# Preparing the operand sums of a third feed-forward unit per layer with accumulating transfers, with other places for the units and their tails

## The chip, the cores and the metric

The kernel runs on one core of one Trainium2 chip. The metric is the device time of one execution in microseconds (us). A core has five engines that run side by side: TensorE (PE in the profile; its weight loads are PEld), VectorE (DVE), ScalarE (ACT), GpSimd (POOL) and SyncE (SP, which only issues transfers). Sixteen DMA engines move data for all of them.

## The reference, cut to what matters

Two layers over 256 positions of width 2048. Layer 0 mixes with pooling and attention, layer 1 with a matrix memory (mLSTM). Each layer ends in the same feed-forward block, which is where the change lies:

```python
def conv_ffn(x, w_up, conv_w, conv_b, w_down):
    u = x @ w_up                                  # 256x2048 @ 2048x11264
    up = jnp.pad(u, ((0, 0), (1, 1), (0, 0)))
    u = c[0] * up[:, :-2] + c[1] * up[:, 1:-1] + c[2] * up[:, 2:] + conv_b
    gate, val = jnp.split(u, 2, axis=-1)
    return (jax.nn.silu(gate) * val) @ w_down     # 256x5632 @ 5632x2048
# every layer: x = x + mixer(rms_norm(x)); x = x + conv_ffn(rms_norm(x), ...)
```

All of it is float32.

## The kernel before

**Products.** A float32 product is made of three reduced products: each weight tile is split into a high part `hl[:, 0]` (a copy that rounds to `fp32r`, line 164, on ScalarE) and a low part `hl[:, 1]` (the difference, line 165, on VectorE), and high x high, high x low and low x high are summed in PSUM (the helper `mm`, line 285). Every weight byte thus passes one ScalarE copy and one VectorE subtraction before TensorE may use it.

**The weight stream.** Class `Stream` walks one list `weights` of 866 chunks of 512 KB in the order in which TensorE will use them. `load` issues chunk i into a raw tile `w` (pool of 6, one more inside the feed-forward block) from SP's queue, `split` makes `hl` from it, `next` hands it to TensorE. TensorE's instructions stand in the order of the code; those of the other engines are ordered by the framework's scheduler when the program is built, except where `keep_in_program_order` pins them.

**Units.** The up-projection has 44 column blocks f, each made of a gate and a value part of 128 columns. Chunks of blocks (`FCH`: 4, 8, 8, 8, 8, 8) alternate with the down-projection of the chunk before. In each of the chunks 2 to 5 the upper half (four blocks) is not multiplied directly but as a *unit* by a seven-product scheme (Strassen's, in Winograd's form, on 2x2 blocks): the generator `quads` runs 8 pairs p; a pair uses sums of weight blocks (b11, b12, b22, b21) and sums of activation blocks (`sx`, made by `sums` on VectorE and ScalarE at the start of the block). A unit therefore saves one product in eight and needs its weight sums from elsewhere. There are two ways to make them:

- *vector units*: chunks marked `sum`, `chain` and `left`; method `Stream.sums` adds them in place in the raw tile on VectorE, four additions of 128x512 for each pair (lines 144, 147, 149, 150), ahead of the split.
- *made units*: `Stream.make_step` prepares a pair in DRAM (tile `G`) in four parts, long ahead. Parts 0 and 1 each copy half of the pair's weights into `G` from SP's queue (line 118, 512 KB) and add to half of it from GpSimd's queue with an accumulating transfer (line 119, 256 KB); parts 2 and 3 each add one piece of `G` to another (line 123, 256 KB). Later `load` reads the finished sums out of `G` (line 93). The dictionary `make` says at which chunk of the stream each part is issued; its entries are made by `_make_steps` from a list of (first chunk, distance between parts).

**Where units stand.** `UNITS` has for each layer four tuples (chunk, half, lo, hi, made). `_ffn_plan` lists the slots of the ordinary work (one slot is one 512 KB chunk, some 2.7 us of TensorE) and weaves the 24 steps of a unit in between slots lo and hi:

```python
UNITS = (
    ((2, 1, 18, 62, 0), (3, 1, 66, 94, 1), (4, 1, 98, 142, 0), (5, 1, 146, 174, 1)),
```

I call them units 2, 3, 4 and 5. Units 2 and 4 are vector units, 3 and 5 made units, in both layers.

**Tails.** When a unit's last product is done, two `finish` generators are queued in the `Weave`, a list of delayed tasks whose clock advances with TensorE's work. Each of them transposes two blocks back (line 1098, four small matrix products), copies them out of PSUM (line 1100) and runs the `tail`: convolution, SiLU, product and split (lines 975 to 984, per block two ScalarE and four VectorE steps of the convolution, then SiLU, a product, a copy and a difference). The set `late` keeps the next unit from starting before all four tails were issued.

Of the kernel before, what the change touches and what calls it, by code (L numbers as in the profile page):

```python
# [237 lines left out]
def trunk(ctx: ExitStack, tc: tile.TileContext, gx, xT, xn, call, catt, cml, weights, make, out):  # L238
# [37 lines left out]
    wv = Weave()  # L276
# [678 lines left out]
    def ffn_layer(layer, norm, nxt):  # L955
        with ExitStack() as es:
# [13 lines left out]
            def tail(u, f, gt, i):  # L970

                y = tp.tile([P, 2, S], F32, tag="y", name=f"y{layer}_{f}")
                for j in range(2):
                    tl = f + j * FT
                    a.activation(y[:, j, :], u[:, j, :], AF.Identity, scale=cw(tl, 1), bias=cw(tl, 3))
                    v.scalar_tensor_tensor(y[:, j, 1:S], u[:, j, 0 : S - 1], cw(tl, 0), y[:, j, 1:S],
                                           ALU.mult, ALU.add)
                    v.scalar_tensor_tensor(y[:, j, 0 : S - 1], u[:, j, 1:S], cw(tl, 2), y[:, j, 0 : S - 1],
                                           ALU.mult, ALU.add)
                s_ = y[:, 0, :]  # L980
                a.activation(s_, s_, AF.Silu)
                v.tensor_mul(s_, s_, y[:, 1, :])
                a.copy(gt[:, i, 0, :], s_)
                v.tensor_sub(gt[:, i, 1, :], s_, gt[:, i, 0, :].bitcast(F32))
# [37 lines left out]
            def product(bank, act, w, c, first, last):  # L1022

                (xh, xl), (wh, wl) = act, (w[:, j, c : c + 512] for j in range(2))
                mm(bank, xh, wh, first, False)
                mm(bank, xh, wl, False, False)
                mm(bank, xl, wh, False, last)
                wv.tick(0.68)

            def block_of(k, t):  # L1030
                return [norm.xx[:, k, j, t * P : t * P + P] for j in range(2)]

            def sum_of(j, p):
                return [sx[:, j, p, i, :] for i in range(2)]

            def quads(fs, c, i0, name):

                def bank(j):
                    return psp.tile([P, 512], F32, tag="ps", name=f"p{j}_{name}")

                def part(j):
                    return cp1.tile([P, 512], F32, tag=f"c{j}", name=f"c{j}_{name}")

                m = KT // 2
                r0, r1 = norm.rcol[:, 0:1], norm.rcol[:, 1:2]
                for p in range(m):
                    ends = p == 0, p == m - 1
                    if p == 0:
                        wv.until(lambda: not late)
                        late.update((0, 2))  # L1050
                    hl = st.next()
                    if p == 0:
                        b1, b5 = bank(1), bank(5)
                    product(b1, block_of(2 * p, 0), hl, 0, *ends)
                    product(b5, sum_of(0, p), hl, 512, *ends)
                    yield
                    hl = st.next()
                    if p == 0:
                        b6, b4 = bank(6), bank(4)
                    product(b6, sum_of(1, p), hl, 0, *ends)  # L1060
                    product(b4, block_of(2 * p + 1, 1), hl, 512, *ends)
                    if p == m - 1:
                        c12, c21, c22 = part(12), part(21), part(22)
                        a.activation(c12, b1, AF.Copy, scale=n0)
                        a.activation(c21, b1, AF.Copy, scale=r1)
                        a.activation(c22, b5, AF.Copy, scale=r1)
                        v.scalar_tensor_tensor(c12, b6, n0, c12, ALU.mult, ALU.add)
                    yield
                for p in range(m):
                    hl = st.next()  # L1070
                    product(b5, sum_of(3, p), hl, 512, False, p == m - 1)
                    product(b6, sum_of(2, p), hl, 0, False, p == m - 1)
                    if p == m - 1:
                        v.scalar_tensor_tensor(c21, b6, r1, c21, ALU.mult, ALU.add)
                        v.tensor_add(c22, c22, c21)
                        v.scalar_tensor_tensor(c21, b4, r1, c21, ALU.mult, ALU.subtract)
                        v.scalar_tensor_tensor(c12, b5, n0, c12, ALU.mult, ALU.add)
                    yield
                    if p % 2:
                        hl = st.next()  # L1080
                        for n in range(2):
                            product(b1, block_of(2 * (p - 1 + n) + 1, 0), hl, n * 512, False, p - 1 + n == m - 1)
                        if p == m - 1:
                            c11 = part(11)
                            a.activation(c11, b1, AF.Copy, scale=r0)
                            gt = g_of(c)
                            wv.add(finish(c12, c22, fs[2:], gt, i0 + 2, name), 3.0)
                            wv.add(finish(c11, c21, fs[:2], gt, i0, name), 5.0)
                        yield

            def finish(top, bottom, fs, gt, i0, name):

                for n, f in enumerate(fs):
                    tr = psp.tile([P, 2, S], F32, tag="ps", name=f"tr{layer}_{f}")
                    for j in range(2):
                        for t, src in enumerate((top, bottom)):
                            c = (2 * j + n) * P
                            pe.transpose(tr[:, j, t * P : t * P + P], src[:, c : c + P], ident)  # L1098
                    u = tp.tile([P, 2, S], F32, tag="tb", name=f"tb_{layer}_{f}")
                    a.copy(u, tr)  # L1100
                    tail(u, f, gt, i0 + n)
                    yield 2.5
                late.discard(i0 % 4)

            def down_end(gt, b, kts):
# [58 lines left out]
            def g_of(c):  # L1164
                if c not in gts:
                    gts[c] = actp.tile([P, 8, 2, S], F32R, tag=f"B{c % 2}", name=f"g{layer}_{c}")
                return gts[c]

            for step in _ffn_plan(layer):
                kind, c = step[:2]  # L1170
                key = step[:3]
                if key not in run:
                    f0 = sum(FCH[:c])
                    run[key] = (up(f0 + step[2], g_of(c), step[2]) if kind == "n" else
                                down(c, gts[c], step[2]) if kind == "d" else
                                quads([f0 + 4 * step[2] + j for j in range(4)], c, 4 * step[2], f"{layer}_{c}{step[2]}"))
                next(run[key], None)
# [64 lines left out]
def _down_chunks(w):  # L1242
# [6 lines left out]


UNITS = (
    ((2, 1, 18, 62, 0), (3, 1, 66, 94, 1), (4, 1, 98, 142, 0), (5, 1, 146, 174, 1)),
    ((2, 1, 18, 62, 0), (3, 1, 66, 94, 1), (4, 1, 98, 142, 0), (5, 1, 146, 174, 1)),
)


# [82 lines left out]
    return out  # L1339


def _make_steps(pairs, places):

    make = {}
    for (key, q), (at, gap) in zip(pairs, places):
        for part in range(4):
            make.setdefault(at + part * gap, []).append((key, part, q))
    return make


def _constants():
# [102 lines left out]
```

## Time and profile before

| | before |
|---|---|
| median of 3 runs | 2180.15 us (2179.67 to 2181.21) |
| the profiled execution's own time | 2179.59 us |
| its span, first to last instruction | 2177.8 us |
| TensorE's granted clock | 1.00 |
| busy: PE / PEld | 2164.5 / 1838.1 us |
| busy: DVE / ACT / POOL | 1711.6 / 1277.6 / 133.5 us |
| moved by DMA | 533.18 MB, mean 245 GB/s |
| share of the 16 DMA engines: SP's queue, GpSimd's queue | 66.2%, 10.5% |

A busy share is an average over stages with different limits. TensorE's matrix products are pipelined, so a small idle time of PE hides in its busy time; the idle time of PEld, its weight loads, and the distance between the starts of two products show it better. Stages, by the span: attention layer until about 254 us, feed-forward block 0 until 977 us, mLSTM layer until 1453 us, feed-forward block 1 until the end.

### The profile page before, as it was taken

How to read it: one execution, taken by the hardware profiler on the slowest of the kernel's cores; microseconds unless marked ns; L12 is line 12 of the kernel's file. 1: busy time of each engine (PE TensorE's matmuls, PEld its weight loads, DVE VectorE, ACT ScalarE, POOL GpSimd, SP SyncE). 2: the span in 40 equal slices, each digit the busy share in tenths (PEclk: the TensorE clock that was granted, in tenths of full speed). 3: DMA queues.
4: the chain of work that ended last, by engine and by line, in shares of the span. 5: the costliest groups of instructions: out<-in, count | busy, mean ns of one | idle time of the engine just before them, and what ended most of it. 6: DMA issues, size and time to landing. Idle time of an engine off the chain costs nothing.

```text
span 2177.8 us, 30504 instructions
## 1 busy us (share of the span) xinstructions
PE 2164.5 (99%) x11040; PEld 1838.1 (84%) x11040; DVE 1711.6 (79%) x2414; ACT 1277.6 (59%) x1808; POOL 133.5 (6%) x168
## 2 busy tenths in 40 slices
PE   9999999999999999999999999999999999999999
PEld 7888888888888888889888888888888888888887
DVE  7686699888798787866767676669888879979785
ACT  7665555666565575655555554556566656556663
POOL 0121101000000000001101010110000000000000
PEclk9999999999999999999999999999999999999999
DMA  8868879889978878769788777877876875767773
GB/s 324 245 217 249 236 234 295 276 264 293 301 235 287 272 232 250 262 202 253 219 248 226 238 229 219 265 223 222 269 244 223 258 247 202 258 232 233 251 232 126
DMA packets 157467, 533.18 MB, mean 245 GB/s; under 512 B 18715, under 2 KB 21059, under 8 KB 156291
## 3 DMA queue, kind: packets, MB, share of 16 engines
q1 hardware_dynamic: 139744, 493.66, 66.2%
q0 software_dynamic: 14496, 33.83, 10.5%
q10 hardware_dynamic: 3074, 3.75, 0.9%
q8 instruction: 86, 1.41, 0.3%
q14 instruction: 67, 0.54, 0.1%
HBM read 529.02 MB, written 69.25 MB: 275 GB/s over the span
## 4 chain that ended last, share of the span: by engine, by line
PE 92%; DVE 6%; issue 1%; ACT 1%; DMA 0%; ACTq 0%; SPq 0%; DVEq 0%
PE up L285 24%; PE dn L285 20%; PE p L285 13%; PE op L285 8%; PE mv L285 4%; PE mq L285 4%; PE mk L285 4%; PE mo L285 4%; PE qproj L285 3%; DVE hl L165 3%; PE pool L285 1%; PE vproj L285 1%; PE kproj L285 1%; ACT hl L164 1%; PE tr L1098 1%
## 5 line engine op out<-in xcount | busy, mean ns | idle before, releaser
L165 DVE TENSOR_TENSOR hl<-w,hl 128x1024 fp32r<-128x1024 f32 (+1 forms) x868 | 1045.0, 1216 | 334.9 <-ACT hl L164 328.1
L164 ACT CAST hl<-w 128x1024 fp32r<-128x1024 f32 (+1 forms) x867 | 897.7, 1048 | 643.7 <-PE up L285 115.8
L285 PE MATMUL up<-xx,hl 128*128 128x512 f32 (+1 forms) x3584 | 647.8, 337 | 0.0
L285 PEld LDWEIGHTS up<-xx,hl 128*128 128x128 f32 x3584 | 563.4, 188 | 87.7 <-DVE hl L165 0.4
L285 PE MATMUL dn<-hl,g 128*128 128x512 f32 x2064 | 492.7, 391 | 0.0
L285 PEld LDWEIGHTS dn<-hl,g 128*128 128x128 f32 x2064 | 385.2, 188 | 78.5
L285 PE MATMUL p<-hl,sx 128*128 128x512 f32 x768 | 206.7, 391 | 3.5 <-DVE hl L165 2.5
L285 PEld LDWEIGHTS p<-hl,sx 128*128 128x128 f32 x768 | 139.4, 188 | 30.6 <-DVE hl L165 3.8
L285 PE MATMUL p<-hl,xx 128*128 128x512 f32 x576 | 157.9, 391 | 4.6 <-DVE hl L165 4.6
L285 PEld LDWEIGHTS p<-hl,xx 128*128 128x128 f32 x576 | 104.5, 188 | 25.3 <-DVE hl L165 6.3
L119 POOL DMA_DIRECT2D G<-in_q x64 | 52.2, 816 | 984.7 <-DMA G<-in_q 972.8
L285 PE MATMUL mk<-xx,hl 128*128 128x512 f32 (+1 forms) x512 | 92.2, 338 | 0.0
L285 PE MATMUL mq<-xx,hl 128*128 128x512 f32 (+1 forms) x512 | 92.2, 338 | 0.0
L285 PE MATMUL mv<-hl,xx 128*128 128x512 f32 (+2 forms) x480 | 91.8, 351 | 0.0
L285 PE MATMUL op<-hl,cat 128*128 128x512 f32 x384 | 91.7, 394 | 0.0
L285 PE MATMUL mo<-hl,xx 128*128 128x512 f32 x384 | 90.6, 392 | 0.0
L285 PE MATMUL op<-hl,mcat 128*128 128x512 f32 x384 | 89.5, 392 | 0.0
L285 PEld LDWEIGHTS mq<-xx,hl 128*128 128x128 f32 x512 | 79.3, 188 | 11.5
L285 PEld LDWEIGHTS mk<-xx,hl 128*128 128x128 f32 x512 | 79.1, 188 | 11.3
L285 PEld LDWEIGHTS mv<-hl,xx 128*128 128x128 f32 x480 | 78.3, 189 | 11.2
L285 PEld LDWEIGHTS op<-hl,mcat 128*128 128x128 f32 x384 | 71.5, 188 | 14.6
L285 PEld LDWEIGHTS mo<-hl,xx 128*128 128x128 f32 x384 | 71.0, 188 | 14.2
(243 smaller groups left out, 1860.8 us busy)
## 6 DMA issues: line engine op xcount, KB each, us to landing
w<-in_up SPq DMA_DIRECT2D x224, 512.0 KB, 4.7
w<-in_dn SPq DMA_DIRECT2D x176, 512.0 KB, 4.6
w<-in_m_in SPq DMA_DIRECT2D x124, 512.0 KB, 5.2
w<-in_q SPq DMA_DIRECT2D x96, 512.0 KB, 4.8
G<-in_q SPq DMA_DIRECT2D x64, 512.0 KB, 5.7
w<-in_a_in SPq DMA_DIRECT2D x46, 512.0 KB, 6.1
G<-in_q POOLq DMA_DIRECT2D x64, 256.0 KB, 6.4
G<-G POOLq DMA_DIRECT2D x64, 256.0 KB, 7.2
```

What stands on the lines that cost most here:

```text
L119: pin(add.dma_start(G[r, 0:1024], src[r, 512:1536], accum_op=ALU.add))
L164: (self.nc.vector.tensor_copy if i + c == 0 else self.nc.scalar.copy)(hl[:, 0, c : c + n], w[:, c : c + n])
L165: self.nc.vector.tensor_sub(hl[:, 1, c : c + n], w[:, c : c + n], hl[:, 0, c : c + n].bitcast(F32))
L285: pe.matmul(out_, lhsT, rhs, start=start, stop=stop, skip_group_check=True)
L1098: pe.transpose(tr[:, j, t * P : t * P + P], src[:, c : c + P], ident)
```

## The change

Unit 2 of both layers becomes a made unit (its last number goes from 0 to 1), so its 32 VectorE additions go and its 8 pairs are prepared in DRAM: 24 pairs per layer list instead of 16. The units get other places: unit 2 ends at slot 57 instead of 62, unit 3 runs from 64 to 90 instead of 66 to 94, unit 4 from 97 to 141 instead of 98 to 142, unit 5 starts at 148 instead of 146. The places of the preparation are new: in layer 0 the 16 pairs of units 2 and 3 start at chunk 24 and then every 9.5 chunks, with 5 chunks between parts, and the 8 pairs of unit 5 every 14 chunks; in layer 1 they start every 13 and every 20 chunks. Before, layer 0 had a pair every 11 chunks for 8 pairs (all of unit 3) and then every 24, and layer 1 every 14. Of the four tails of a unit, the second pair is queued 11.0 instead of 5.0 us after the unit, and the two of a pair lie 4.0 instead of 2.5 us apart.

```diff
-                            wv.add(finish(c11, c21, fs[:2], gt, i0, name), 5.0)
+                            wv.add(finish(c11, c21, fs[:2], gt, i0, name), 11.0)
...
                     tail(u, f, gt, i0 + n)
-                    yield 2.5
+                    yield 4.0
...
 UNITS = (
-    ((2, 1, 18, 62, 0), (3, 1, 66, 94, 1), (4, 1, 98, 142, 0), (5, 1, 146, 174, 1)),
...
+    ((2, 1, 18, 57, 1), (3, 1, 64, 90, 1), (4, 1, 97, 141, 0), (5, 1, 148, 174, 1)),
...
-    make = _make_steps(pairs[0], [(24 + 11 * k, 5) for k in range(8)] + [(len(att) + 30 + 24 * k, 12) for k in range(8)])
-    make.update(_make_steps(pairs[1], [(len(weights) - 20 + 14 * k, 7) for k in range(16)]))
+    places = [[(24 + 19 * k // 2, 5) for k in range(16)] + [(len(att) + 110 + 14 * k, 7) for k in range(8)]]
+    at = len(weights) + len(ml)
+    places.append([(at - 182 + 13 * k, 6) for k in range(16)] + [(at + 26 + 20 * k, 10) for k in range(8)])
+    make = {}
+    for l in range(2):
+        _make_steps(make, pairs[l], places[l])
```

(`_make_steps` now fills the dictionary that it is given; what it writes is the same. `att` and `ml` are the chunk lists of the two mixers, with 80 and 162 entries; a feed-forward block has 312.)

What the built program makes of it shows in three places.

SP's queue in feed-forward block 0, around chunk 152. Rows L118 are the copies into `G` (G031_5 is pair 5 of layer 0's unit 3, G051 belongs to unit 5); all others are loads of the stream. Before:

```order
L100 DMA w155_3983<-in_up0 128x1024
L100 DMA w156_3994<-in_q0 128x1024
L100 DMA w157_4031<-in_dn0 128x1024
L100 DMA w158_4052<-in_q0 128x1024
L118 DMA G051_2_4055<-in_q0 16x8192
L100 DMA w159_4067<-in_dn0 128x1024
L100 DMA w160_4089<-in_up0 128x1024
L100 DMA w161_4100<-in_b0 128x1024
L100 DMA w162_4122<-in_up0 128x1024
```

The same place now:

```order
L93 DMA w152_3928<-in_q0 128x512
L118 DMA G031_5_3831<-in_q0 16x8192
L100 DMA w153_3943<-in_up0 128x1024
L93 DMA w154_3965<-G021_5_2146 128x512
L93 DMA w154_3965<-in_q0 128x512
L100 DMA w155_3977<-in_up0 128x1024
L100 DMA w156_3998<-in_b0 128x1024
L100 DMA w157_4019<-in_up0 128x1024
L118 DMA G031_6_4022<-in_q0 16x8192
L100 DMA w158_4034<-in_up0 128x1024
```

While unit 2 runs, copies now follow each other after every four to six chunks; between chunks 100 and 180 there were 8 of them and are 16. Each copy brings two accumulating transfers on GpSimd's queue.

VectorE in the same block, a few chunks into unit 2. Rows L165 are the subtractions of the split, L144, L149 and L150 the additions of a vector unit, the rest ordinary tails (y, g, tb_up). Before:

```order
L144 TENSOR_TENSOR w108_3059<-w108_3059 128x512
L982 TENSOR_TENSOR y0_4_3048<-y0_4_3048 128x256
L165 TENSOR_TENSOR hl109_3160<-w109_3073,hl109_3160 128x1024
L165 TENSOR_TENSOR hl108_3139<-w108_3059,hl108_3139 128x1024
L165 TENSOR_TENSOR hl110_3171<-w110_3098,hl110_3171 128x1024
L149 TENSOR_TENSOR w111_3114<-w111_3114,w108_3059 128x512
L984 TENSOR_TENSOR g0_1_2930<-y0_4_3048,g0_1_2930 128x256
L450 TENSOR_TENSOR tb_up0_5_3192<-up0_5_3072,tb_up0_5_3192 128x512
L150 TENSOR_TENSOR w111_3114<-w111_3114 128x512
L994 TENSOR_TENSOR tb_up0_5_3192<-tb_up0_5_3192,R1_2576 128x512
L165 TENSOR_TENSOR hl111_3209<-w111_3114,hl111_3209 128x1024
```

Now:

```order
L165 TENSOR_TENSOR hl108_3143<-w108_3064,hl108_3143 128x1024
L976 SCALAR_TENSOR_TENSOR y0_4_3053<-tb_up0_4_3049,cst_84,y0_4_3053 128x255 x2
L165 TENSOR_TENSOR hl109_3154<-w109_3079,hl109_3154 128x1024
L984 TENSOR_TENSOR g0_0_2461<-y0_3_2926,g0_0_2461 128x256
L978 SCALAR_TENSOR_TENSOR y0_4_3053<-tb_up0_4_3049,cst_84,y0_4_3053 128x255 x2
L165 TENSOR_TENSOR hl110_3177<-w110_3105,hl110_3177 128x1024
L165 TENSOR_TENSOR hl111_3214<-w111_3119,hl111_3214 128x1024
L982 TENSOR_TENSOR y0_4_3053<-y0_4_3053 128x256
L450 TENSOR_TENSOR tb_up0_5_3196<-up0_5_3078,tb_up0_5_3196 128x512
```

The additions are gone, and subtractions and tails are left.

TensorE after the end of layer 0's unit 2: rows L1098 are the transposes of the tails (tr0_16 is block 16), the others ordinary products. Before:

```order
L1098 MATMUL tr0_16_4444<-cst_84,c11_0_21_4390 128x128
L1098 MATMUL tr0_16_4444<-cst_84,c21_0_21_3736 128x128
L1098 MATMUL tr0_16_4444<-cst_84,c11_0_21_4390 128x128
L1098 MATMUL tr0_16_4444<-cst_84,c21_0_21_3736 128x128
L285 MATMUL dn0_1_0_4360<-hl171_4381,g0_1_2930 128x512 x6
L1098 MATMUL tr0_19_4474<-cst_84,c12_0_21_3735 128x128
```

Now, after the same tail:

```order
L1098 MATMUL tr0_16_4441<-cst_84,c11_0_21_4286 128x128
L1098 MATMUL tr0_16_4441<-cst_84,c21_0_21_3686 128x128
L285 MATMUL dn0_1_0_4429<-hl168_4316,g0_1_2937 128x512 x6
L285 MATMUL dn0_1_0_4429<-hl169_4356,g0_1_2937 128x512 x12
L285 MATMUL dn0_1_0_4429<-hl170_4395,g0_1_2937 128x512 x6
L1098 MATMUL tr0_17_4495<-cst_84,c11_0_21_4286 128x128
```

Six products stood between two tails, now 24; the transposes themselves are the same.

More of the change, by code (lines that the diff above doesn't have):

```diff
@@ L1251 @@
 UNITS = (
-    ((2, 1, 18, 62, 0), (3, 1, 66, 94, 1), (4, 1, 98, 142, 0), (5, 1, 146, 174, 1)),
-    ((2, 1, 18, 62, 0), (3, 1, 66, 94, 1), (4, 1, 98, 142, 0), (5, 1, 146, 174, 1)),
+    ((2, 1, 18, 57, 1), (3, 1, 64, 90, 1), (4, 1, 97, 141, 0), (5, 1, 148, 174, 1)),
+    ((2, 1, 18, 57, 1), (3, 1, 64, 90, 1), (4, 1, 97, 141, 0), (5, 1, 148, 174, 1)),
 )
@@ L1339, in _with_prep, with _make_steps @@
     return out
-def _make_steps(pairs, places):
-    make = {}
+def _make_steps(make, pairs, places):
     for (key, q), (at, gap) in zip(pairs, places):
@@ L1347, in _make_steps @@
             make.setdefault(at + part * gap, []).append((key, part, q))
-    return make
 def _constants():
```

## Prediction

> **What bounds the kernel now.** I read the page's head and the chain first, then the waits of TensorE's weight loads, then a table of stages. From the page, with the costliest VectorE group:
>
> ```profile
> span 2177.8 us, 30504 instructions
> PE 2164.5 (99%) x11040; PEld 1838.1 (84%) x11040; DVE 1711.6 (79%) x2414; ACT 1277.6 (59%) x1808; POOL 133.5 (6%) x168
> PE 92%; DVE 6%; issue 1%; ACT 1%; DMA 0%; ACTq 0%; SPq 0%; DVEq 0%
> L165 DVE TENSOR_TENSOR hl<-w,hl 128x1024 fp32r<-128x1024 f32 (+1 forms) x868 | 1045.0, 1216 | 334.9 <-ACT hl L164 328.1
> ```
>
> TensorE sets the time. No transfer is on the chain, but VectorE's subtractions (L165) are, although VectorE is busy only 79% on average. The waits of the weight loads (total us, times, longest us) say where:
>
> ```profile
> PEld p L285 <- DVE hl L165: 10.1, 10, 2.0
> PEld p L285 <- ACT hl L164: 1.4, 2, 0.9
> ```
>
> Only products `p`, those of the units, wait noticeably, and mostly for the low half of a weight. The stages (us, busy time by engine, clock, DMA share, GB/s) are unit 2 of layer 0, unit 2 of layer 1, the made unit 3 of layer 0, unit 4 of layer 0, unit 4 of layer 1:
>
> ```profile
> 310.00:462.00 152.00, 150.03 (x778) 127.02 (x777) 134.78 (x181) 90.52 (x117) 10.53 (x13) 1.00 0.85 277
> 1509.00:1643.00 134.00, 129.98 (x677) 110.23 (x677) 118.20 (x159) 79.35 (x104) 4.04 (x5) 1.00 0.75 246
> 472.00:593.00 121.00, 121.00 (x602) 102.25 (x601) 95.21 (x121) 76.74 (x100) 8.15 (x10) 1.00 0.91 290
> 609.00:767.00 158.00, 156.67 (x779) 132.34 (x777) 134.41 (x176) 90.47 (x114) 8.93 (x11) 1.00 0.85 270
> 1790.00:1948.00 158.00, 157.15 (x776) 132.66 (x776) 137.65 (x185) 94.49 (x124) 0.00 (x0) 1.00 0.68 230
> ```
>
> TensorE idles 1.97, 4.02, 0, 1.33 and 0.85 us there. The vector units lose time with VectorE at 85 to 89%; the made unit, with VectorE at 79%, loses none. How a loss comes about shows in the timeline of the worst wait, VectorE and then TensorE (start, us; idle before and releaser in brackets):
>
> ```profile
> 1516.67 0.41 DVE L982 TENSOR_TENSOR y<-y 128x256 f32<-128x256 f32 x1
> 1517.01 0.67 DVE L149 TENSOR_TENSOR w<-w,w 128x512 f32<-128x512 f32 x1
> 1517.61 0.67 DVE L994 TENSOR_TENSOR tb_up<-tb_up,R 128x512 f32<-128x512 f32 x1
> 1518.21 2.34 DVE L165 TENSOR_TENSOR hl<-w,hl 128x1024 fp32r<-128x1024 f32 x2
> 1517.37 0.39 PE L285 MATMUL p<-hl,xx 128*128 128x512 f32 x1
> 1519.47 0.72 PE L285 MATMUL p<-hl,xx 128*128 128x512 f32 x2 [1.71 <-DVE hl L165]
> ```
>
> A tail (L982), an addition of the unit (L149) and a conversion (L994) stand ahead of the subtraction that TensorE wants. It is a local queue on VectorE, not a late transfer.
>
> **The change part by part.** *Removable stall.* The five windows give 1.97 + 4.02 + 1.33 + 0.85 = 8.2 us as a lower bound, since a short stop hides in pipelined busy time; the weight loads' waits give 10.1 + 1.4 = 11.5 us as the upper. Unit 2 has 5.99 of the 8.17, or 73%: 6.0 to 8.4 us, and I take 7.2. Unit 4 has the rest, 2.2 to 3.1, and I take 2.6.
>
> *The additions.* Their groups, with two steps of a tail:
>
> ```profile
> L144 DVE TENSOR_TENSOR w<-w 128x512 f32<-128x512 f32 x32 | 21.8, 682 | 0.0
> L147 DVE TENSOR_TENSOR w<-w 128x512 f32<-128x512 f32 x32 | 21.9, 683 | 0.0
> L149 DVE TENSOR_TENSOR w<-w,w 128x512 f32<-128x512 f32 x32 | 21.8, 682 | 0.0
> L150 DVE TENSOR_TENSOR w<-w 128x512 f32<-128x512 f32 x32 | 21.9, 683 | 0.2
> L976 DVE SCALAR_TENSOR_TENSOR y<-tb,cst,y 128x255 f32<-128x255 f32 x64 | 28.4, 476 | 0.0
> L982 DVE TENSOR_TENSOR y<-y 128x256 f32<-128x256 f32 x88 | 36.6, 416 | 0.6 <-ACT y L981 0.6
> ```
>
> Of 128 additions 64 go, 64 x 0.683 = 43.7 us, 21.9 per layer. Unit 2's window in layer 0 then needs (134.78 - 21.9) / 152 = 74% of VectorE. Unit 2 now takes 39 instead of 44 slots, which makes it somewhat denser; but unit 3 packs the same steps into 28 slots, has 79% and loses nothing, so I count the whole 7.2 us as gained. None of the 43.7 us is gained as such, since TensorE is the bound. What is late next would be the split's copy on ScalarE, 60% busy there.
>
> *Tails.* Four tails of a unit cost VectorE 4 x (4 x 0.476 + 2 x 0.416) = 10.9 us. They stood 6 products apart, under 2 us of TensorE, and now 24, so they no longer come as one burst. Unit 4 keeps its additions; only the tails that run into its start lie thinner. That helps its first waits and not its later ones: half of 2.6, 1.3 us (bounds 0 and 3.1). The second pair is queued 6.0 us later and ends 3 us later still; what needs it, the down-projection of the same chunk, comes tens of slots later except after unit 5, whose results feed the last down-projection. There the added 9 us eat slack; if it were gone, TensorE would wait at most that long, once per layer, and I count nothing. Moving units by a few slots changes no work. Gain so far: 7.2 + 1.3 = 8.5 us.
>
> *Transfers.* Each layer gets 16 more copies on SP's queue and 32 more accumulating transfers on GpSimd's. What matters is where they pile up: chunks 100 to 180 of layer 0, 285 to 473 us, with copies going from 8 to 16 and accumulating transfers from 17 to 33. DMA view of this window (queues; then issues with count, size, median landing), and the denser slices of 20 us:
>
> ```profile
> q1 hardware_dynamic: 11942, 45.80, 68.6%
> q0 software_dynamic: 1937, 4.46, 15.6%
> DMA packets 13892, 50.43 MB, mean 268 GB/s; under 512 B 1703, under 2 KB 1703, under 8 KB 13751
> G<-in_q SPq DMA_DIRECT2D x8, 512.0 KB, 6.0
> G<-G POOLq DMA_DIRECT2D x9, 256.0 KB, 7.9
> G<-in_q POOLq DMA_DIRECT2D x8, 256.0 KB, 6.3
> 20.00:40.00 20.00, 20.00 (x90) 16.58 (x89) 15.36 (x23) 15.41 (x39) 0.00 (x0) 1.00 1.03 410
> 340.00:360.00 20.00, 19.59 (x106) 16.63 (x106) 18.86 (x24) 10.85 (x15) 1.47 (x3) 1.00 0.97 318
> 700.00:720.00 20.00, 20.00 (x100) 16.88 (x100) 15.34 (x21) 11.37 (x14) 0.76 (x1) 1.00 0.94 312
> ```
>
> By time: SP's queue takes 0.686 x 188 = 129 us of the 16 engines for 45.80 MB, so a copy of 0.524 MB takes 1.48 us; GpSimd's takes 0.156 x 188 = 29.3 us for 17, so 1.73 us each. Added: 8 x 1.48 + 16 x 1.73 = 39.5 us, 21% of 188. The share would rise from 85 to 105.5%, which is more than there is. By bytes: 8 x 0.524 + 16 x 0.262 = 8.39 MB at the 410 GB/s of the first slice is 20.5 us, 10.9%, and the share becomes 95%. The truth lies between: part of a packet's time is waiting beside others, but accumulating packets are dearer than plain ones. The rate would be (50.43 + 8.39) MB / 188 us = 313 GB/s, what the two mixed slices reach for 20 us (318 and 312), while unit 3's window holds 290 for 121 us with TensorE never idle. So it is tight, not clearly too much. Bounds: 0, if the raw tiles and the lead of the prepared pairs swallow it, and 10.3 us, if 198.3 us of transfers must pass in 188. I take 1.5 us, near the lower end, because the rows nearest to it (0.91, 0.94 and 1.03 of DMA with no idle TensorE) lost nothing. Layer 1's unit 2 has a share of 0.75, and its copies are spread from 182 chunks ahead of the block on, so I charge nothing there.
>
> The wait that this adds: a load from `G` waits on SP for the pair's last part, and all later loads of the stream stand behind it. The last part of the tightest pair (the last of unit 3) is placed at chunk 181 and first read for chunk 198. At 2177.8 us / 866 chunks = 2.51 us these 17 chunks are 43 us, against 8 us for landing: covered until transfers run late by some 35 us.
>
> *GpSimd.* Its 64 more issues are of these kinds:
>
> ```profile
> L119 POOL DMA_DIRECT2D G<-in_q x64 | 52.2, 816 | 984.7 <-DMA G<-in_q 972.8 <-issue 11.9
> L123 POOL DMA_DIRECT2D G<-G x64 | 59.1, 923 | 177.7 <-DMA G<-in_q 132.7 <-DMA G<-G 38.7 <-issue 6.2
> L119 POOL DMA_DIRECT2D G<-in_q x8: 778/790/792, 296.2 to 459.0; - x8
>   DVE re_n L294: 2.6, 3
> ```
>
> They add 64 x 0.87 = 56 us to an engine that is busy 6%. Behind an issue that waits for its copy stand only the few square roots of the norms (ry), for which VectorE waited 2.6 us in all (last row); I charge nothing, at most another 2.6. The third row shows the issues in unit 2's window (shortest, median, longest ns): 778 to 792 while VectorE is 89% busy, so VectorE does not hold them up here. The Trainium skill's page "SBUF — State Buffer" (section "Reading the diagram") speaks against more of them: it says that GpSimd writes the descriptors of such a transfer, that some VectorE operations lock it out of the memory port meanwhile, and that one took some 3.1 us instead of 0.62. By that page each added issue would be some 2.3 us longer, as an estimate, and the sum at most some 5 us higher where the square roots stand behind them; the narrow spread in the row disagrees.
>
> *Sum.* 2179.59 - 8.5 + 1.5 = 2172.6 us for a profiled execution. The median of the runs lies 0.56 above the profiled one, so 2173.2 us.
>
> **The rivals.** Where the measurement can tell a difference is about 0.2%, 4.4 us: below 2175.8 is faster, above 2184.5 slower.
>
> *B, no change that can be told.* The waits sit at the units' starts, where tails and conversions cross, and stay there without the additions. For it: in the quoted timeline the addition is 0.67 us of a queue of 4.1 us. Against it: unit 3 has the same tails ahead of it and loses nothing. If half of unit 2's 7.2 us stays and unit 4 gains nothing, the time is 2179.59 - 3.6 + 1.5 + 0.56 = 2178.0.
>
> *C, slower: the 16 engines are oversubscribed in 285 to 473 us.* Transfers of 105.5% at the 97% that the fullest mixed slice shows need 204.5 us, so TensorE waits 16.5 us for raw weights at loads around chunks 100 to 200. Layer 0's gain at unit 2, some 2.5 us, goes too. 2179.59 - 6.0 + 16.5 + 0.56 = 2190.7. It decides from a loss of 10.4 us on, that is about where the share needed reaches 100%. For it speaks the sum by time, against it that no transfer is on the chain now and that 290 GB/s cost nothing.
>
> *D, much slower: memory traffic is the limit, not the engines.* A copy and an accumulating transfer move their bytes more than once: read and written for a copy, two reads and a write for an accumulating one. In 188 us there would be 80 loads of 0.524 (41.9 MB), 16 x 1.05 and 33 x 0.79: 84.8 MB, 451 GB/s. If memory gave only the highest rate seen, 410, they would need 207 us, 19 more than there are: 2179.59 - 6.0 + 19 + 0.56 = 2193. The Trainium skill's page "DMA: Bandwidth & Descriptors" (section "Specifications") gives about 358 GB/s of memory per core; by it, as an estimate, 237 us would be needed, and the time would be 2223. The slice at 410 GB/s, with TensorE busy 20.00 of 20 us, is above this limit and disagrees for this core alone.
>
> **How the numbers follow.** The forecast 0.58: its mechanism is seen in every vector unit and absent in the made one. B 0.21. C 0.18, because one of two ways of counting the transfers ends above what there is. D 0.03. The range: its lower end is the whole 11.5 us gone at no price, 2179.59 - 11.5 + 0.56 = 2168.6, so 2168.5; its upper end takes in B and the part of C below 2189, the lower three quarters of its 10.3 to 16.5 us. Left out are the rest of C, D and a little below: under 0.15. The forecast's own range is 2168.5 to 2176. Faster 0.58, same 0.21, slower 0.18 + 0.03 = 0.21.
>
> **What would show it.** Right: in the waits of the weight loads, `p` behind L165 falls from 10.1 to under 4 us, none of it in unit 2; the groups L144 to L150 have half their counts and VectorE's busy time is some 44 us less; DMA shares in 285 to 473 us stay below 1.0 and no product waits for a transfer or for a subtraction that itself waited for `w`. Wrong: `p` behind L165 remains near 7 us in the unit 2 windows (B); or VectorE's and ScalarE's split waits for `w` by DMA for several us between 285 and 500 us with a DMA share near 1.0 (C, D); or the last down-projection waits for tails of unit 5.

## The result and the profile after

The changed kernel takes 2171.27 us (median of 5 runs, 2171.08 to 2172.01); the kernel before, run beside it, 2180.8 us. The ratio is 0.9959, 95% interval [0.9947, 0.9971], that is 6 to 12 us less. The profiled execution took 2171.85 us against 2179.59, 7.7 us less. The profiled execution of the kernel before is at the fast end of its runs (2179.67 to 2181.27), so the medians lie 9.5 us apart; the terms below are held against the 7.7 us. The kernel before, run beside each group of experiments below, took 2180.8 to 2181.8 us, so a difference of under 1 us between runs of different groups says little by itself.

From the page of the changed kernel, its head and its chain:

```profile
span 2170.1 us, 30692 instructions
PE 2162.6 (100%) x11040; PEld 1838.7 (85%) x11040; DVE 1679.4 (77%) x2350; ACT 1285.1 (59%) x1808; POOL 185.5 (9%) x232
PE 98%; DVE 1%; issue 0%; ACT 0%; DMA 0%; ACTq 0%; DVEq 0%
```

VectorE's share of the chain fell from 6% to 1%. The waits of the weight loads:

```profile
PEld p L285 <- DVE hl L165: 2.8, 3, 1.1
PEld p L285 <- ACT hl L164: 1.1, 1, 1.1
```

11.5 us of waits of products `p` have become 3.9, 7.6 less: all but 0.1 us of the difference of the two profiled executions. All 3.9 us that are left lie in layer 1's unit 4. The stages follow, in the order layer 0's chunks 100 to 180, unit 2 of layer 0, unit 2 of layer 1, unit 4 of layer 0, unit 4 of layer 1. As in the prediction, a row gives the stretch, its length, the busy time of TensorE, weight loads, VectorE, ScalarE and GpSimd, the clock, the DMA share and GB/s:

```profile
285.00:473.00 188.00, 188.00 (x995) 161.12 (x994) 158.16 (x215) 121.15 (x164) 27.50 (x34) 1.00 1.00 322
310.00:462.00 152.00, 152.00 (x797) 130.16 (x796) 123.64 (x159) 95.49 (x123) 22.67 (x28) 1.00 1.02 334
1509.00:1643.00 134.00, 134.00 (x697) 114.49 (x696) 106.24 (x136) 82.74 (x105) 9.76 (x12) 1.00 0.94 294
600.00:760.00 160.00, 160.00 (x797) 135.53 (x796) 135.88 (x176) 90.43 (x112) 15.39 (x19) 1.00 0.93 291
1790.00:1948.00 158.00, 155.67 (x764) 130.38 (x763) 132.99 (x178) 88.66 (x113) 4.89 (x6) 1.00 0.76 244
```

Unit 2 idles nowhere now, and neither does layer 0's unit 4; layer 1's unit 4 idles 2.33 us where it was 0.85. The DMA engines in layer 0 are at 1.00 to 1.02 of their time, and TensorE idles nowhere in these rows; no weight load waits there either.

### The profile page after: what moved, and what is told of

Same layout as the page of the kernel before. It is cut to its first block, busy times and chain, and to the rows that moved or that the text cites. A ratio compares the mean times of both kernels' runs of the same rounds, so it can differ in the third digit from the quotient of the medians.

```text
span 2170.1 us, 30692 instructions
## 1 busy us (share of the span) xinstructions
PE 2162.6 (100%) x11040; PEld 1838.7 (85%) x11040; DVE 1679.4 (77%) x2350; ACT 1285.1 (59%) x1808; POOL 185.5 (9%) x232
## 4 chain that ended last, share of the span: by engine, by line
PE 98%; DVE 1%; issue 0%; ACT 0%; DMA 0%; ACTq 0%; DVEq 0%
PE up L285 28%; PE dn L285 21%; PE p L285 14%; PE op L285 8%; PE mv L285 4%; PE mq L285 4%; PE mk L285 4%; PE mo L285 4%; PE qproj L285 3%; PE pool L285 1%; PE kproj L285 1%; PE vproj L285 1%; PE tr L1098 1%; PE av L285 1%; PE qk L285 1%; PE end L285 1%
## 5 line engine op out<-in xcount | busy, mean ns | idle before, releaser
L165 DVE TENSOR_TENSOR hl<-w,hl 128x1024 fp32r<-128x1024 f32 (+1 forms) x868 | 1049.8, 1218 | 344.9 <-ACT hl L164 336.7
L119 POOL DMA_DIRECT2D G<-in_q x96 | 77.0, 802 | 1177.3 <-DMA G<-in_q 1165.7
L123 POOL DMA_DIRECT2D G<-G x96 | 89.2, 929 | 258.6 <-DMA G<-in_q 180.8
L285 PEld LDWEIGHTS mq<-xx,hl 128*128 128x128 f32 x512 | 79.4, 188 | 11.5
L285 PEld LDWEIGHTS mk<-xx,hl 128*128 128x128 f32 x512 | 79.2, 188 | 11.3
```

Source lines behind the costliest of these rows:

```text
L119: pin(add.dma_start(G[r, 0:1024], src[r, 512:1536], accum_op=ALU.add))
L123: pin(add.dma_start(G[:, at : at + 512], G[:, of : of + 512], accum_op=ALU.add))
L165: self.nc.vector.tensor_sub(hl[:, 1, c : c + n], w[:, c : c + n], hl[:, 0, c : c + n].bitcast(F32))
L285: pe.matmul(out_, lhsT, rhs, start=start, stop=stop, skip_group_check=True)
```

## The experiments

**The tails alone, and the change without them.** The first run undoes the tails:

```diff
-  wv.add(finish(c11, c21, fs[:2], gt, i0, name), 11.0)
+  wv.add(finish(c11, c21, fs[:2], gt, i0, name), 5.0)
...
-                    yield 4.0
+                    yield 2.5
```

> The changed kernel with the old tails (second pair after 5.0 us, 2.5 us apart); unit 2 stays a made unit and the slots stay new. Theory (the removed additions are what counts): unit 2 still loses nothing, only unit 4's start in layer 0 may lose up to 1.5 us again: 2171 to 2173 us. Rival (the thinner tails are what counts): the waits at the starts of units come back, 2175 us or more.

Measured: 2170.79 us (2170.60 to 2171.64), as fast as the changed kernel or a little faster. Unit 4 of layer 1 waits 3.1 us in it instead of 3.9, and layer 0's unit 4 still not at all. The second run has the tails alone, on the kernel before (the same two lines the other way round):

> The kernel before with the new tails alone (11.0 and 4.0 us). Theory: unit 2 has its additions and its waits, so 2179 to 2181 us, at most 1.5 us less from unit 4. Rival (tails): most of the 9 us is there, 2172 to 2175 us.

Measured: 2183.96 us, ratio 1.0009 [1.0001, 1.0018], which neither expected: the tails alone cost a little. The waits of the weight loads in its profile:

```profile
PEld p L285 <- DVE hl L165: 11.2, 11, 2.5
PEld mq L285 <- DVE hl L165: 1.6, 2, 0.9
```

Nothing of the 10.1 us is gone, 1.1 us came at the units (all at units 4), and 1.6 us at products of layer 1's mixer (`mq`), 1002 us into the span or later. The profiled execution (2184.00) is 4.4 us longer than the one before, which is more than these waits; its granted clock was 0.999 against 1.000. The tails are not where the gain comes from.

**The additions alone.** In the kernel before, unit 2's blocks go unsummed into the split, in both layers; its additions are left out, nothing is prepared for it, and slots and tails stay:

```diff
+            if c == 2:
+                seq.append(q[:, 512:1536] if n >= 2 * m else q[:, 1024:2048] if n % 2 else q[:, 0:1024])
-            if n >= 2 * m:
+            elif n >= 2 * m:
```

> The kernel before with the 32 additions of unit 2 left out in both layers: the raw blocks go into the split, nothing is prepared in their place, and slots and tails are as before. Theory: the waits of unit 2 vanish by themselves, 3.5 to 5 us in each layer, and unit 4's remain: 2171 to 2173.5 us. Rival (it takes the new tails or slots): 2176 us or more.

Measured: 2171.31 us (2170.69 to 2173.10), ratio 0.9955 [0.9941, 0.9969]. That is the time of the changed kernel, without its transfers, its slots and its tails. The waits for VectorE (none for ScalarE is left), then the two stages of unit 2 and the two of unit 4:

```profile
PEld p L285 <- DVE hl L165: 2.9, 2, 1.8
```

```profile
310.00:462.00 152.00, 152.00 (x796) 129.97 (x795) 119.60 (x153) 92.57 (x117) 10.55 (x13) 1.00 0.89 281
1509.00:1643.00 134.00, 134.00 (x701) 114.58 (x700) 106.98 (x139) 82.04 (x106) 4.04 (x5) 1.00 0.79 255
609.00:767.00 158.00, 156.67 (x773) 132.16 (x772) 134.32 (x174) 91.81 (x115) 8.93 (x11) 1.00 0.86 270
1790.00:1948.00 158.00, 157.15 (x781) 132.76 (x780) 137.37 (x183) 91.69 (x119) 0.00 (x0) 1.00 0.71 231
```

Unit 2's loss is gone to the last 0.01 us, and unit 4's 1.33 and 0.85 us are exactly those of before. So of the 11.5 us of waits 8.6 belong to unit 2 and 2.9 to unit 4, and the profiled execution (2170.86) is 8.7 us shorter. The kernel before says the same of unit 2 when its weight loads' waits are taken over 300 to 470 us (layer 0, first two rows) and 1500 to 1650 us (layer 1):

```profile
PEld p L285 <- DVE hl L165: 2.7, 4, 1.1
PEld p L285 <- ACT hl L164: 0.5, 1, 0.5
PEld p L285 <- DVE hl L165: 4.5, 4, 2.0
PEld p L285 <- ACT hl L164: 0.9, 1, 0.9
```

**One layer.** Unit 2 is made in layer 1 alone; layer 0 has units and places of before, and the new tails stay:

```diff
-    ((2, 1, 18, 57, 1), (3, 1, 64, 90, 1), (4, 1, 97, 141, 0), (5, 1, 148, 174, 1)),
+    ((2, 1, 18, 62, 0), (3, 1, 66, 94, 1), (4, 1, 98, 142, 0), (5, 1, 146, 174, 1)),
...
-    places = [[(24 + 19 * k // 2, 5) for k in range(16)] + [(len(att) + 110 + 14 * k, 7) for k in range(8)]]
+    places = [[(24 + 11 * k, 5) for k in range(8)] + [(len(att) + 30 + 24 * k, 12) for k in range(8)]]
```

> Unit 2 is a made unit in layer 1 only; layer 0 has the units, slots and places of preparation of before, but the new tails. Theory: layer 0's unit 2 loses its 3 to 4 us again and layer 1's does not, so about half of the gain: 2174.5 to 2176.5 us. Rival (tails): 2171 to 2173 us.

Measured: 2178.51 us, ratio 0.9985 [0.9976, 0.9994]: less gain than half, and slower than either expectation. Its waits and its two feed-forward blocks:

```profile
PEld p L285 <- DVE hl L165: 7.7, 8, 2.5
PEld p L285 <- ACT hl L164: 1.7, 2, 1.2
```

```profile
254.00:977.00 723.00, 718.95 (x3626) 608.32 (x3625) 606.49 (x813) 442.48 (x589) 41.79 (x52) 1.00 0.84 262
1453.00:2175.70 722.70, 716.75 (x3607) 606.35 (x3605) 582.42 (x765) 433.19 (x562) 32.16 (x40) 1.00 0.80 251
```

Layer 0 idles 4.05 us in its block, all of its old loss (3.29 us) and more: the longest wait, at unit 4, is 2.5 us as with the tails alone, where it was 1.7 us before. Layer 1 got rid of unit 2's waits and loses more at unit 4, 3.6 us of waits instead of 1.2. Waits of 9.4 us against 11.5 are 2.1 less, and the profiled execution, 2177.48, is 2.1 less.

**The slots.** Unit 2 is made in both layers, and the slots are those of before, first in both layers, then in layer 1 only:

```diff
-    ((2, 1, 18, 57, 1), (3, 1, 64, 90, 1), (4, 1, 97, 141, 0), (5, 1, 148, 174, 1)),
+    ((2, 1, 18, 62, 1), (3, 1, 66, 94, 1), (4, 1, 98, 142, 0), (5, 1, 146, 174, 1)),
```

> The changed kernel with the slots of the units as before (unit 2 from 18 to 62, unit 3 from 66 to 94, unit 4 from 98 to 142, unit 5 from 146); unit 2 is still a made unit. Theory: 2170 to 2173 us, the slots carry nothing at unit 2. Rival (the slots count): 2175 us or more.

> The changed kernel with the new slots in layer 0 and the slots of before in layer 1 (unit 2 made in both). If the slots decide what unit 4 loses, layer 1's unit 4 loses 1.0 us as with the old slots instead of 3.1, and layer 0's nothing: 2169 to 2169.8 us. If it is something else (the places of preparation, the new tails): 2171 to 2172 us.

Measured: 2172.28 us (2172.09 to 2173.57) and 2169.71 us (2169.69 to 2170.03). The waits with the old slots in both layers, then with the mixture; neither has one for ScalarE at products `p`:

```profile
PEld p L285 <- DVE hl L165: 4.0, 3, 2.5
PEld p L285 <- DVE hl L165: 1.5, 2, 1.2
```

Units 4 of layer 0 and layer 1 with the old slots in both, then with the mixture:

```profile
600.00:760.00 160.00, 157.92 (x791) 133.51 (x790) 136.05 (x180) 93.00 (x119) 15.43 (x19) 1.00 0.93 289
1790.00:1948.00 158.00, 157.15 (x778) 132.36 (x777) 137.05 (x184) 92.25 (x119) 5.69 (x7) 1.00 0.80 249
```

```profile
600.00:760.00 160.00, 160.00 (x797) 135.46 (x796) 135.91 (x176) 90.58 (x112) 15.42 (x19) 1.00 0.92 291
1790.00:1948.00 158.00, 157.15 (x781) 132.52 (x780) 135.87 (x182) 91.75 (x119) 4.90 (x6) 1.00 0.80 251
```

So the new slots clear layer 0's unit 4 (2.08 us idle with the old, 0 with the new) and harm layer 1's (0.85 with the old, 2.33 with the new). By the waits it is more: layer 0's slots alone part the two runs here, 4.0 us against 1.5, and layer 1's slots alone part the mixture from the changed kernel, 1.5 us against 3.9. VectorE has nearly the same work in all of them (133 to 137 us), so the amount of work does not decide. What is left is when VectorE comes to a subtraction, measured against TensorE; that is shown below for one place and only argued for the others. The worst of these waits, layer 0's unit 4 with the old slots and the new tails, on VectorE and on TensorE:

```profile
629.58 1.22 DVE L165 TENSOR_TENSOR hl<-w,hl 128x1024 fp32r<-128x1024 f32 x1
630.71 0.68 DVE L149 TENSOR_TENSOR w<-w,w 128x512 f32<-128x512 f32 x1
631.31 0.48 DVE L978 SCALAR_TENSOR_TENSOR y<-tb_up,cst,y 128x255 f32<-128x255 f32 x1
631.71 1.22 DVE L165 TENSOR_TENSOR hl<-w,hl 128x1024 fp32r<-128x1024 f32 x1
```

```profile
632.98 0.73 PE L285 MATMUL p<-hl,xx 128*128 128x512 f32 x2 [2.08 <-DVE hl L165]
```

An addition of unit 4 and a step of the convolution of an ordinary block (`tb_up`) stand between two subtractions, and TensorE waits for the second of them. The same place in the kernel before, with the old tails:

```profile
635.60 0.73 PE L285 MATMUL p<-hl,xx 128*128 128x512 f32 x2 [1.33 <-DVE hl L165]
```

The four rows stand on VectorE in the same order there; with the new tails VectorE comes to them 0.75 us later against TensorE. Which tail puts it back was not followed further up.

**How near the transfers are to their limit.** For each of the 16 pairs of layer 0's units 2 and 3 one half, 512 KB, is copied once more, to a place that nothing reads; in the second kernel both halves are (`part < 2`), twice as many:

```diff
             pin(sync.dma_start(G[r], src[r]))
+            if key[:2] in ("02", "03") and part < 1:
+                X = self.dpool.tile([64, 2048], F32, tag=f"X{key}{part}", name=f"X{key}{part}")
+                pin(sync.dma_start(X, src[r]))
```

> The changed kernel with one more 512 KB copy to an unused place for each of the 16 pairs of layer 0's units 2 and 3, 8 of them between 285 and 473 us. The DMA share there was 1.00 and would have to be about 1.06 by the 1.48 us of a copy. Theory that DMA time is the limit at 1.00: about 11 us slower, 2180 to 2185 us. Rival (the share counts waiting packets, and bytes are the limit at 410 GB/s): 345 GB/s, no more than 1 us slower, 2171 to 2172.5 us.

> The same with two more copies for each pair, 16 between 285 and 473 us. DMA time as the limit: some 22 us slower, 2190 to 2196 us. Bytes at 410 GB/s: 367 GB/s wanted, 2171 to 2174 us. If the limit lies between, this one is clearly slower and the one with 8 is not.

Measured: 2174.74 us (2174.00 to 2177.06), 3.5 more than the changed kernel, and 2189.5 us (2188.61 to 2191.20), 18.2 more. The window 285 to 473 us, the first kernel and then the second, with the wait of ScalarE's split in the second (in these two kernels every later code line has a number higher by three):

```profile
285.00:473.00 188.00, 186.39 (x982) 158.57 (x981) 152.87 (x205) 116.64 (x157) 25.94 (x32) 1.00 1.02 333
```

```profile
285.00:473.00 188.00, 177.20 (x905) 146.64 (x904) 141.01 (x186) 105.46 (x141) 24.32 (x30) 0.99 1.02 328
```

```profile
ACT hl L167 <- DMA w<-in_up: 33.0, 15, 4.3
```

Over the whole window, share and rate do not rise any more, at 1.02 and 328 to 333 GB/s (single slices of 20 us reach up to 382), and from there each copy in the window lengthens the program. The copies ahead of the window, as many again, cost nothing: TensorE idles 0 us from 20 to 285 us in both kernels. 0.524 MB at 333 GB/s is 1.57 us, so 8 copies in the window should cost 12.6 us; the second eight cost 14.8, the first eight 3.5 (2.6 by the weight loads' waits, 6.5 us against 3.9). As an estimate, the changed kernel thus stands about 9 us of transfers, 5% of the window, below the point from which each further copy costs its full time. With 16 more copies the program is slower than before (ratio 1.0038 [1.0025, 1.0050]), in the way C says.

**A faster version.** The only waits of units left are those of layer 1's unit 4. It is made as well, in layer 1 alone:

```diff
-    ((2, 1, 18, 57, 1), (3, 1, 64, 90, 1), (4, 1, 97, 141, 0), (5, 1, 148, 174, 1)),
+    ((2, 1, 18, 57, 1), (3, 1, 64, 90, 1), (4, 1, 97, 141, 1), (5, 1, 148, 174, 1)),
...
-    places.append([(at - 182 + 13 * k, 6) for k in range(16)] + [(at + 26 + 20 * k, 10) for k in range(8)])
+    places.append([(at - 182 + 13 * k, 6) for k in range(16)] + [(at + 26 + 12 * k, 6) for k in range(8)] + [(at + 120 + 12 * k, 7) for k in range(8)])
```

> The changed kernel with unit 4 of layer 1 made in DRAM too: 32 more additions leave VectorE, 16 more copies and 32 more accumulating transfers come to layer 1, whose DMA share is 0.80. The changed kernel loses 3.1 us at that unit. Theory: they go, 2168 to 2169.5 us. Rival (layer 1's transfers are then too many, or the waits come from tails alone): 2171 us or more.

Measured: 2168.36 us (2168.26 to 2168.59), ratio 0.9940 [0.9927, 0.9952]. No product `p` waits any more, and unit 4 of layer 1 runs through, at a DMA share of 0.97:

```profile
1790.00:1948.00 158.00, 158.00 (x784) 133.66 (x783) 118.60 (x147) 92.34 (x116) 18.02 (x22) 1.00 0.97 304
```

With the old tails on top:

> Unit 4 of layer 1 made too, and the old tails (5.0 and 2.5 us). The run with unit 4 made lost nothing at any unit, so if the tails act only through the waits of units: 2168.0 to 2168.8 us, the same as with the new tails. If the new tails cost time elsewhere (the changed kernel was 0.5 us faster with the old ones): 2167 to 2167.9 us.

Measured: 2169.15 us (2169.06 to 2169.40), 0.8 us more, which neither expectation covers. No product `p` waits here either. The last additions of the output (L1130), with the new tails and with the old:

```profile
2162.57 0.69 DVE L1130 TENSOR_TENSOR x<-x,end 128x512 f32<-128x512 f32 x1 [0.67 <-PE end L285]
```

```profile
2162.24 0.69 DVE L1130 TENSOR_TENSOR x<-x,end 128x512 f32<-128x512 f32 x1 [0.67 <-PE end L285]
```

With the old tails the computation ends 0.3 us earlier and the span is 0.8 us longer (2167.3 against 2166.5), so 1.1 us come after it, in the last store: from the end of the last addition to the end of the span it is 4.4 us here and 3.2 in the run with the new tails. It is 3.2 us too in the changed kernel with the old tails, so the old tails alone do not lengthen the store. What does is open.

## Why the prediction was right, and where its terms were off

**Right.** The time (2173.2 forecast, 2171.27 measured), the direction, and the mechanism: VectorE's additions in unit 2 make TensorE wait, and without them unit 2 loses nothing. The run without additions shows that by itself, and the tails alone do not give it.

**Unit 2: 7.2 us forecast, 8.6 measured.** The removable stall was split between the units by the idle time of TensorE in the windows, 73% for unit 2. By the run without additions it is 8.6 of 11.5, 75%, and the weight loads' waits are the right measure of the total: 7.6 us fewer waits went with 7.7 us less time in the changed kernel, 8.6 with 8.7 without the additions, 2.1 with 2.1 in one layer, 7.5 with 7.4 and 10.0 with 9.9 in the two runs on the slots, 8.4 with 8.7 with the old tails, 11.5 with 11.3 in the faster version. My lower bound from busy time of TensorE counted too little, and the middle of the two was not the better choice. The waits over unit 2's windows give 8.6 us from the profile before alone.

**Unit 4: 1.3 us gain forecast, 1.0 us loss measured (2.9 us of waits before, 3.9 after).** This step failed. I gave the thinner tails half of unit 4's waits. Tails alone made them longer (1.7 to 2.5 us at layer 0's unit 4, 1.2 to 1.5 at layer 1's); what moved unit 4 most was the slots, to which I gave no price at all ("Moving units by a few slots changes no work"). The amount of work is unchanged, but the waits are not: by them the slots are worth 2.5 us in layer 0 and 2.4 us, with the other sign, in layer 1.

**Transfers: 1.5 us forecast, 0 measured.** The row of 285 to 473 us has TensorE at 188.00 of 188, and no weight load waits there. Their load lay between the two ways of counting, share 1.00 (105.5% by time, 95% by bytes at 410 GB/s). The queues and the loads from `in_up`, and last the same loads in the kernel before:

```profile
q1 hardware_dynamic: 15108, 51.59, 73.5%
q0 software_dynamic: 3828, 8.82, 26.6%
w<-in_up SPq DMA_DIRECT2D x37, 512.0 KB, 9.0
w<-in_up SPq DMA_DIRECT2D x37, 512.0 KB, 5.6
```

An accumulating transfer takes 0.266 x 188 / 34 = 1.47 us of the sixteen engines instead of 1.73, and a load lands after 9.0 us instead of 5.6 (median), without a wait of TensorE. Rival C was nearer than its 0.18 suggests: eight more copies cost 3.5 us, sixteen turn the result round.

**The sum** is right by errors that cancel: 7.2 + 1.3 - 1.5 = 7.0 us forecast; 8.6 - 1.0 - 0 = 7.6 by the waits, 7.7 by the profiled executions. That the forecast came so near is partly luck. Of the 1.9 us between 2173.2 and 2171.27, 0.7 are from the terms; the rest comes from the step from the profiled execution to the median, which the forecast put at 0.56 us up and which was 0.58 us down.

**What was to be seen.** `p` behind L165 fell to 2.8 us, under 4, none in unit 2, as said. No product waits for a transfer. VectorE's busy time fell by 32.2 us, not 44, although 64 instructions are gone as counted: neighbours overlap. In the timeline that the prediction shows, the addition lasts 0.67 us and the next instruction starts after 0.60, so 64 of them free, as an estimate, some 38 us; and the group of the subtractions counts 4.8 us more than before (1045.0), for which no run shows the reason:

```profile
L165 DVE TENSOR_TENSOR hl<-w,hl 128x1024 fp32r<-128x1024 f32 (+1 forms) x868 | 1049.8, 1218 | 344.9 <-ACT hl L164 336.7
```

The DMA share was to stay below 1.0 and did not, without harm.

**The other rivals.** B is out: no wait is left at unit 2's start. D is out for what was at stake: its accounting wanted 451 GB/s of memory traffic in the window, and the window held it with no idle TensorE. If an accumulating transfer moves its bytes as D counts them, that is also above the 358 GB/s of the Trainium skill's page "DMA: Bandwidth & Descriptors" (section "Specifications"), for this one core. GpSimd's issues beside VectorE stayed as short as before:

```profile
L119 POOL DMA_DIRECT2D G<-in_q x16: 778/790/792, 293.7 to 457.1; - x16
```

```profile
  DVE re_n L294: 2.6, 3
```

There are twice as many, 778 to 792 ns each, and the square roots keep VectorE waiting the same 2.6 us. Nothing of the 2.3 us more for each issue that the prediction estimated shows; it had no row that says whether VectorE's operations here are of the kind that locks GpSimd out.

## What to carry to other kernels

When a unit's own work on a side engine makes the main engine wait, leaving that work out prices the gain before anybody builds the replacement: here 8.7 us, of which the finished change kept 7.7. Where the load of a side engine is the same and the waits are not, a shift by a few slots can be worth nearly as much as moving that engine's work (here 2.4 to 2.5 us, with either sign, against 3.2 and 5.4 us for unit 2's additions in the two layers), and has to be tried place by place. Before work is moved to transfers, load them with useless copies until the time rises: that tells how much room there is, and a busy share of 1.00 does not.

## What was not expected of the hardware

The share of the DMA engines reads 1.00 to 1.02 both in the changed kernel, which loses nothing, and in the one with 16 more copies, which loses 18 us; landing times tell more (loads from `in_up` between 285 and 473 us: 5.6 us before, 9.0 in the changed kernel, 11.1 with 8 more copies, 12.4 with 16). With this mix of loads, copies and accumulating transfers the rate over 150 us and more ends at 328 to 334 GB/s, although plain loads reached 410 for 20 us at the start of the program. Waits of the weight loads of products `p` add up to the lost time within 0.3 us in seven pairs of kernels with a granted clock of 1.000, and the busy time of the matrix products does not: it fell by 1.9 us where the program became 7.7 us shorter. The run with the longer last store misses by its 1.1 us, and the one with the tails alone, at a clock of 0.999, does not add up.
